# Attention in a hybrid block: later transposes, and operand splits spread over the query blocks

## The chip, the cores and the metric

The kernel runs on one core of a Trainium2 chip. The metric is the time of one execution in device microseconds (us). Three runs of the kernel before took 2177.57, 2182.42 and 2185.70 us; the median is 2182.42 us. A separate execution was profiled.

## The reference, cut to what matters

The block has a gated DeltaNet branch, an attention branch (MLA), a merge and a gated MLP. Only the attention's inner part bears on the change:

```python
# 8 heads, S = 1024 positions, keys of 128 + 64 channels, values of 128, f32
for s0 in range(0, S, 128):                      # 8 query blocks
    s1 = s0 + 128
    kb, vb = k[:, :s1], v[:, :s1]                # block-causal: keys up to s1
    sc = einsum('bqhd,bkhd->bhqk', q[:, s0:s1], kb) * scale
    sc = where(mask, sc, -inf)                   # mask by chunks of 64
    p = softmax(sc)
    outs.append(einsum('bhqk,bkhd->bqhd', p, vb))
```

## The kernel before, in words

All matrix products are done in a fast float32 form (fp32r) on operands that are split into a high and a low part. A product of two split operands takes three matmuls (high by high, high by low, low by high).

**The attention, in units.** A unit is one head and one query block of 128 rows. `units` lists, for each head, the blocks 6, 7, 0, 1, 4, 5, 2, 3 (`PAIRS`, L1200). For a unit with block i there are three jobs:

- `qk_ops` (L1212): scores, (i+1) x 128 columns wide, in PSUM banks of 512. Each bank takes five matmuls `s`: three over the 128 plain channels (`qnh`, `qnl`, `knh`, `knl`), two over the rotary channels (`qst` by `kst`, `qst` by `klo`). VectorE (DVE) takes the row maximum `nm` of each bank (L1233) and, with two banks, the smaller of the negated maxima (L1238). ScalarE (ACT) writes the exponentials into the SBUF tile `P` (L1240). DVE adds the row sums `sm` of two banks (L1242) and inverts them (L1243). GpSimd (POOL) multiplies `P` by the inverse (L136). There is one `P` tile for each of the eight blocks, and there are four score banks.
- `t_ops` (L1249): TensorE (PE) transposes `P` in chunks of up to four 128 x 128 tiles into a bank `pT` (L66). ACT copies the bank out as the high part `PTh` (L1263), DVE writes the low part `PTl` (L1264). There are two `pT` banks, so a chunk's transposes wait until the `PTl` of the chunk two before it is done.
- `pv_ops` (L1270): for a pair of blocks, the product with the values, matmuls `o`.

**Their order on PE** is written out by `attend`: step j issues the scores of unit j, the transposes of unit j - `LT`, and half of the value product of a pair whose last unit is `LT + LV` steps old. `LT` and `LV` are 4. A gate (`TD0`, `TD1`) keeps the transposes from being placed sooner than an assumed delay after their scores. `PEOrder` pins PE to that order. Each engine works through its own queue in order.

**The next head's operands.** While head h is under way, `attend` issues the loads for head h+1: `load_qk` for `kn`, `qn`, `kst`, `qst`, and `load_v`. `LJ` (L1177) says at which block of head h each of the four is issued; the entries are 0, 0, 0, 0, that is, all at the head's first step. Each load is a DMA on SP's queue into one of three raw buffers, and then a split: `knh`, `kst`, `qst` and `vh` are made by POOL (about 1 us each), `knl`, `qnl` and `vl` by POOL, `qnh` by ACT, and `klo` and the lower half of `qst` by DVE (L1192). The tiles of even heads have one buffer of each name, so `knh` of head 4 can be written only after head 2's last scores. For head 1 the entries are always 0, whatever `LJ` holds.

The order of the queues of DVE, ACT, POOL and SP is not the order of the program text: a scheduler places each instruction, and picks a raw buffer for each load, by its own estimates. It may place a split a whole head before the one that it is issued in.

Of the kernel before, what the change touches and what calls it, by code (L numbers as in the profile page):

```python
# [108 lines left out]
def build(tc, A, out):  # L109
    nc = tc.nc  # L110
    with ExitStack() as ctx:
        _body(tc, nc, ctx, A, out)


def _body(tc, nc, ctx, A, out):
# [1058 lines left out]
            nc.sync.dma_start(o(raw), src)  # L1174
        return raw

    LJ = (0, 0, 0, 0)  # L1177

    def load_qk(h, n):
        LOP = 3 if h != 1 else 0  # L1180
# [19 lines left out]
    PAIRS = (3, 0, 2, 1)  # L1200
    units = [(h, p, 2 * p + u) for h in range(NH) for p in PAIRS for u in range(2)]
    NU = len(units)
    LT = 4
    LV = 4
    TD0 = 3.5
    TD1 = 3e-3
# [3 lines left out]
    def qk_ops(j):  # L1210
        h, p, i = units[j]
        qc = slice(i * P, i * P + P)  # L1212
        W = (i + 1) * P
        nb = (W + 511) // 512
        d = hd[h]
        Pt = Pts[j] = pm.tile([P, W], F32, tag=f"P{i}", name=f"P{h}_{i}")
        nm = pm.tile([P, 2], F32, tag="nm", bufs=8, name=f"nm{h}_{i}")
        sm = pm.tile([P, 2], F32, tag="sm", bufs=8, name=f"sm{h}_{i}")
        ts = []

        def bank_op(b):
            w = min(512, W - b * 512)
            kc = slice(b * 512, b * 512 + w)
            t = bank("wk", f"s{h}_{i}_{b}")
            o = t[:, 0:w]
            pe.mm(o, d["qnh"][:, qc], d["knh"][:, kc], True, False)
            pe.mm(o, d["qnh"][:, qc], d["knl"][:, kc], False, False)
            pe.mm(o, d["qnl"][:, qc], d["knh"][:, kc], False, False)
            pe.mm(o, d["qst"][:, qc], d["kst"][:, kc], False, False)
            pe.mm(o, d["qst"][:, qc], d["klo"][:, kc], False, True)  # L1230
            if b == nb - 1:
                nc.vector.memset(t[0:64, w - 64:w], -1.0e30)
            nc.vector.tensor_reduce(nm[:, b:b + 1], o, axis=AX.X, op=ALU.max, negate=True)  # L1233
            ts.append((o, kc))
            if b < nb - 1:
                return
            if nb == 2:
                nc.vector.tensor_tensor(nm[:, 0:1], nm[:, 0:1], nm[:, 1:2], op=ALU.min)  # L1238
            for b, (o, kc) in enumerate(ts):
                nc.scalar.activation(Pt[:, kc], o, AF.Exp, bias=nm[:, 0:1], accum_out=sm[:, b:b + 1])  # L1240
            if nb == 2:
                nc.vector.tensor_tensor(sm[:, 0:1], sm[:, 0:1], sm[:, 1:2], op=ALU.add)  # L1242
            nc.vector.reciprocal(sm[:, 0:1], sm[:, 0:1])  # L1243
            gmul(Pt, Pt, sm[:, 0:1])
            pe.mark("QK", j)

        return [lambda b=b: bank_op(b) for b in range(nb)]

    def t_ops(j):  # L1249
        h, p, i = units[j]  # L1250
        n2 = j // 2
        u = i % 2
        if u == 0:
            PTs[n2] = [pm.tile([P, 2 * p + 2, 256], F32R, tag=f"PT{n}{p}", name=f"PT{n}{h}_{p}") for n in "hl"]
        PTh, PTl = PTs[n2]

        def chunk(k0):
            n = min(4, i + 1 - k0)
            t = bank("tp", f"pT{h}_{i}_{k0}")
            transposes(t, [Pts[j][:, (k0 + m) * P:(k0 + m + 1) * P] for m in range(n)])  # L1260
            tv = t[:, 0:n * P].rearrange("p (k c) -> p k c", c=P)
            dh = PTh[:, k0:k0 + n, u * P:(u + 1) * P]
            nc.scalar.copy(dh, tv)  # L1263
            nc.vector.tensor_tensor(PTl[:, k0:k0 + n, u * P:(u + 1) * P], tv, dh.bitcast(F32), op=ALU.subtract)  # L1264

        return [lambda k0=k0: chunk(k0) for k0 in range(0, i + 1, 4)]
# [36 lines left out]
    def attend():  # L1303
# [4 lines left out]
        pvq, nv = [], 1  # L1308
        for j in range(NU + LT + LV + 4):
            if j < NU:  # L1310
                h = units[j][0]
                if h == 1 and j % 8 == 0:
                    yield ((("ya",),), 0.0)
                for n, at in zip(("kn", "qn", "kst", "qst"), LJ if h else (0, 0, 0, 0)):
                    if h < NH - 1 and j % 8 == at:
# [3 lines left out]
            qs = qk_ops(j) if j < NU else []  # L1319
            ts = t_ops(j - LT) if 0 <= j - LT < NU else []  # L1320
            jv = j - LT - LV
            if 0 <= jv < NU and jv % 2 == 1:
# [5 lines left out]
            for r in range(n):  # L1328
# [6 lines left out]
                if r < len(ts):  # L1335
                    if r == 0:
                        yield ((("QK", j - LT),), TD0 + TD1 * (units[j - LT][2] + 1) * P)
                    ts[r]()
# [494 lines left out]
```

## Time and profile before

| | |
|---|---|
| median of three runs | 2182.42 us |
| the profiled execution | 2181.9 us |
| its span | 2180.2 us |
| PE busy in the span | 2085.7 us (96%) |
| DVE / ACT / POOL busy | 1334.7 / 903.8 / 735.2 us |
| attention: first scores of head 1 to last transposes after head 7's scores | 1128.26 to 1304.90 us |

The share of PE is an average over the whole block; the attention's stretch is read by itself in windows, one window to a head. A window starts with the head's first score matmul. A head's window also holds the previous head's transposes and value products, so that each whole head has the same work on PE.

### The profile page before, as it was taken

The page shows a single profiled execution, that of the slowest core. Times are in us where ns is not written, and L with a number is a line of the kernel's source. Part 1 is how long each engine was busy: PE and PEld are TensorE (multiplying, and loading weights), DVE is VectorE, ACT ScalarE, POOL GpSimd, SP SyncE. Part 2 cuts the span into 40 slices and gives each one's busy share as a digit, 9 for nine tenths or more (in the row PEclk, how much of TensorE's full clock was granted, in tenths as well). Part 3 has the DMA queues.
Part 4 walks back from the last instruction along what each step waited for, and adds up shares of the span by engine and source line. Part 5 has one row for each costly group of instructions (what it writes and reads, how often), then busy time and mean ns, then how long its engine had stood idle before and what let it go on. Part 6 is the DMA issues. An engine that isn't in the chain of part 4 may idle for free.

```text
span 2180.2 us, 30681 instructions
## 1 busy us (share of the span) xinstructions
PE 2085.7 (96%) x11526; PEld 1800.2 (83%) x11526; DVE 1334.7 (61%) x2214; ACT 903.8 (41%) x1822; POOL 735.2 (34%) x544
## 2 busy tenths in 40 slices
PE   6999999999999999889999999999999999999999
PEld 5878778888888899888778888898788888878887
DVE  7586798345565428677458885626665555564553
ACT  5666213443554423245136663246343433332222
POOL 1033320211101214447357760317544444442221
PEclk8999999999999999999999999999999999999999
DMA  9477523334333237687744427423322222344644
GB/s 272 124 196 197 147 88 131 90 90 125 107 117 93 82 111 240 201 299 243 237 146 130 126 69 256 131 88 97 111 93 78 87 87 87 95 143 145 222 146 148
DMA packets 277462, 309.31 MB, mean 142 GB/s; under 512 B 38896, under 2 KB 218429, under 8 KB 277057
## 3 DMA queue, kind: packets, MB, share of 16 engines
q1 hardware_dynamic: 277312, 307.35, 45.4%
q8 instruction: 91, 1.49, 0.3%
q14 instruction: 59, 0.48, 0.1%
HBM read 223.63 MB, written 83.66 MB: 141 GB/s over the span
## 4 chain that ended last, share of the span: by engine, by line
PE 70%; DVE 13%; DMA 8%; issue 3%; ACT 3%; POOL 3%; SPq 1%; ACTq 0%; DVEq 0%; POOLq 0%
PE d L63 11%; PE gt L63 5%; PE m L63 5%; PE my L63 5%; PE mx L63 5%; PE yb L63 4%; PE v L63 4%; PE wo L63 4%; PE qt L63 4%; PE q L63 3%; PE s L63 3%; PE mz L63 2%; PE ya L63 2%; DMA wada<-in_w_ada 2%; PE zt L63 2%
## 5 line engine op out<-in xcount | busy, mean ns | idle before, releaser
L63 PE MATMUL d<-wd,gh 128*128 128x512 f32 x704 | 217.5, 390 | 2.2 <-DVE wd L151 1.7
L63 PEld LDWEIGHTS d<-wd,gh 128*128 128x128 f32 x704 | 132.1, 188 | 30.7 <-DVE wd L151 2.5
L63 PE MATMUL d<-wd,gl 128*128 128x512 f32 x352 | 137.0, 389 | 0.0
L139 POOL TENSOR_TENSOR wdr<-wdr,gf 128x512 f32<-128x512 f32 x44 | 69.7, 1585 | 162.2 <-DMA wdr<-in_ffn_w_down 150.6
L151 DVE TENSOR_TENSOR gl<-gr,gh 128x1024 fp32r<-128x1024 f32 x44 | 56.3, 1281 | 109.7 <-ACT gh L143 107.6
L143 ACT CAST gh<-gr 128x1024 fp32r<-128x1024 f32 x44 | 46.3, 1054 | 153.4 <-PE d L63 152.9
L63 PEld LDWEIGHTS d<-wd,gl 128*128 128x128 f32 x352 | 66.1, 188 | 13.8
L1240 ACT ACTIVATE P<-s,nm 128x512 f32<-128x512 f32 (+2 forms) x96 | 55.3, 582 | 53.1 <-DVE nm L1238 44.4
L139 POOL TENSOR_TENSOR acc<-acc,vv 128x512 f32<-128x512 f32 x44 | 65.0, 1496 | 20.6 <-ACT acc L1768 20.6
L136 POOL TENSOR_SCALAR P<-P,sm 128x896 f32<-128x896 f32 (+4 forms) x64 | 49.7, 783 | 63.5 <-DVE nm L1238 16.7
L621 DVE TENSOR_TENSOR lt<-X 128x62 f32<-128x62 f32 (+30 forms) x62 | 61.6, 994 | 15.4 <-DMA X<-bd_d 13.3
L623 DVE TENSOR_TENSOR X<-X,lt 128x62 f32<-128x62 f32 (+30 forms) x62 | 61.8, 996 | 2.0
L1122 DVE SCALAR_TENSOR_TENSOR ada<-wada,sc,ada 128x1024 f32<-128x1024 f32 x28 | 42.5, 1518 | 32.7 <-DMA wada<-in_w_ada 32.6
L151 DVE TENSOR_TENSOR wd<-wdr,wd 128x512 fp32r<-128x512 f32 x44 | 61.2, 1392 | 1.8 <-ACT wd L143 1.8
L63 PE MATMUL mz<-T2h,wP 128*128 128x512 f32 x176 | 59.1, 397 | 3.1 <-ACT wP L143 2.1
L66 PE MATMUL pT<-ident,P 128*128 128x128 f32 x288 | 49.5, 282 | 12.7 <-DVE PTl L1264 9.6
L1263 ACT CAST PTh<-pT 128x512 fp32r<-128x512 f32 (+2 forms) x96 | 46.0, 484 | 37.6 <-PE pT L66 37.3
L63 PE MATMUL m<-B21h,wP 128*128 128x512 f32 x176 | 59.6, 400 | 0.0
L63 PE MATMUL mx<-B22h,wP 128*128 128x512 f32 x176 | 57.9, 390 | 0.0
L63 PE MATMUL my<-T4h,wP 128*128 128x512 f32 x176 | 57.8, 389 | 0.0
L63 PE MATMUL my<-T3h,wP 128*128 128x512 f32 x176 | 57.8, 389 | 0.0
L63 PE MATMUL m<-B11h,wP 128*128 128x512 f32 x176 | 57.5, 389 | 0.0
(1429 smaller groups left out, 7214.7 us busy)
## 6 DMA issues: line engine op xcount, KB each, us to landing
gr<-gg_d SPq DMA_DIRECT2D x44, 512.0 KB
wada<-in_w_ada SPq DMA_DIRECT2D x32, 512.0 KB
gg_d<-acc SPq DMA_DIRECT2D x22, 512.0 KB
wdr<-in_ffn_w_down SPq DMA_DIRECT2D x44, 256.0 KB
x<-in_x SPq DMA_DIRECT2D x16, 512.0 KB
ad<-in_w_ada SPq DMA_DIRECT2D x16, 512.0 KB
sg_d<-gst SPq DMA_DIRECT2D x32, 256.0 KB
q_d<-qst SPq DMA_DIRECT2D x48, 128.0 KB
```

What stands on the lines that cost most here:

```text
L63: self._pin(self.nc.tensor.matmul(out, lhsT, rhs, start=start, stop=stop, skip_group_check=more), cost)
L66: self._pin(self.nc.tensor.transpose(out=out, in_=in_, identity=ident), 0.107)
L136: return nc.gpsimd.tensor_scalar(o, i, by, 0.0, op0=ALU.mult, op1=ALU.add)
L139: nc.gpsimd.tensor_tensor(o, a, b, op=op)
L143: nc.scalar.copy(hi, src)
L151: return nc.vector.tensor_tensor(lo, src, hi.bitcast(F32), op=ALU.subtract)
L621: nc.vector.tensor_tensor(tv, X[:, 0:k, k:k + 1].broadcast_to([P, k, n]), X[:, k:k + 1, k + 1:64].broadcast_to([P, k, n]), op=ALU.mult)
L623: nc.vector.tensor_tensor(X[:, 0:k, k + 1:64], X[:, 0:k, k + 1:64], tv, op=ALU.add)
L1122: nc.vector.scalar_tensor_tensor(acc, raw, sc[:, k:k + 1], acc, op0=ALU.mult, op1=ALU.add)
L1240: nc.scalar.activation(Pt[:, kc], o, AF.Exp, bias=nm[:, 0:1], accum_out=sm[:, b:b + 1])
L1263: nc.scalar.copy(dh, tv)
```

## The change

`LJ` becomes 0, 1, 3, 5: of the next head's operands `kn` is issued at block position 0, `qn` at 1, `kst` at 3 and `qst` at 5. `LT` becomes 6: the transposes of a unit stand six steps behind its scores, and the value products, which hang on `LT + LV`, ten steps behind in place of eight.

```diff
-    LJ = (0, 0, 0, 0)
+    LJ = (0, 1, 3, 5)
@@
-    LT = 4
+    LT = 6
```

No instruction is added or removed on PE, DVE, ACT or POOL; all are the same in kind and number, and stand in another order.

On PE, from the opening of head 3 (`s3_6_0` is the first score bank of head 3, block 6; `pT2_4_0` the first chunk of head 2, block 4; the last matmul of each bank is shown). Before:

```order
L63 MATMUL s3_6_0_11079<-klo3_10729,qst3_10735 128x512
...
L66 MATMUL pT2_4_0_11089<-ident_73,P2_4_10902 128x128 x4
...
L63 MATMUL s3_7_0_11129<-klo3_10729,qst3_10735 128x512
...
L66 MATMUL pT2_5_0_11142<-ident_73,P2_5_10945 128x128 x4
...
L66 MATMUL pT2_2_0_11204<-ident_73,P2_2_10993 128x128 x3
```

Now:

```order
L63 MATMUL s3_6_0_11032<-klo3_10818,qst3_10909 128x512
...
L66 MATMUL pT2_0_0_11042<-ident_73,P2_0_10776 128x128
...
L63 MATMUL s3_7_0_11077<-klo3_10818,qst3_10909 128x512
...
L66 MATMUL pT2_1_0_11087<-ident_73,P2_1_10824 128x128 x2
...
L63 MATMUL s3_0_0_11114<-klo3_10818,qst3_10909 128x128
...
L66 MATMUL pT2_4_0_11128<-ident_73,P2_4_10863 128x128 x4
...
L66 MATMUL pT2_5_0_11178<-ident_73,P2_5_10915 128x128 x4
```

The wide score blocks 6 and 7 now stand beside the narrow transposes of blocks 0 and 1, and the wide transposes of 4 and 5 beside the narrow scores of 0 and 1.

On DVE in head 3, around the low half of head 4's `qst`. Before:

```order
L1264 TENSOR_TENSOR PTl2_2_11078<-pT2_5_0_11142,PTh2_2_11077 128x4x128
L1238 TENSOR_TENSOR nm3_7_11126<-nm3_7_11126 128x1
L1264 TENSOR_TENSOR PTl2_2_11078<-pT2_5_4_11169,PTh2_2_11077 128x2x128
L1232 MEMSET s3_0_0_11179 64x64
L1233 TENSOR_REDUCE nm3_0_11175<-s3_0_0_11179 128x1
L1192 TENSOR_TENSOR qst4_11068<-qstr4_11069,qst4_11068 64x1024
```

Now:

```order
L1238 TENSOR_TENSOR nm3_7_11074<-nm3_7_11074 128x1
L1192 TENSOR_TENSOR qst4_11242<-qstr4_11243,qst4_11242 64x1024
L1233 TENSOR_REDUCE nm3_0_11110<-s3_0_0_11114 128x1
L1232 MEMSET s3_1_0_11161 64x64
L1242 TENSOR_TENSOR sm3_7_11075<-sm3_7_11075 128x1
L1233 TENSOR_REDUCE nm3_1_11158<-s3_1_0_11161 128x1
L1243 RECIPROCAL sm3_7_11075<-sm3_7_11075 128x1
L1264 TENSOR_TENSOR PTl2_2_11113<-pT2_4_0_11128,PTh2_2_11112 128x4x128
```

`qst4` stood behind the copies of block 5's transposes; now the copies of blocks 4 and 5 stand behind it. Later in the same head DVE now also has head 5's `klo5` and `qst5`, the latter just ahead of the copies of blocks 6 and 7:

```order
L1233 TENSOR_REDUCE nm3_2_11284<-s3_2_0_11288 128x1
L1192 TENSOR_TENSOR qst5_11575<-qstr5_11576,qst5_11575 64x1024
L1264 TENSOR_TENSOR PTl3_3_11287<-pT3_6_0_11299,PTh3_3_11286 128x4x128
L1264 TENSOR_TENSOR PTl3_3_11287<-pT3_6_4_11310,PTh3_3_11286 128x3x128
```

In the kernel before they stand in head 4. On POOL, at the change from head 2 to head 3 (`P2_5` is the scaling of head 2, block 5). Before:

```order
L136 TENSOR_SCALAR knh4_11049<-knr4_11051 128x1024
L136 TENSOR_SCALAR kst4_11061<-kstr4_11063 128x1024
L136 TENSOR_SCALAR P2_2_10993<-P2_2_10993,sm2_2_10995 128x384
L139 TENSOR_TENSOR qnl4_11056<-qnr4_11057,qnh4_11055 128x1024
L139 TENSOR_TENSOR knl4_11050<-knr4_11051,knh4_11049 128x1024
L136 TENSOR_SCALAR P2_3_11023<-P2_3_11023,sm2_3_11025 128x512
L136 TENSOR_SCALAR qst4_11068<-qstr4_11069 128x1024
```

Now:

```order
L136 TENSOR_SCALAR knh4_11021<-knr4_11023 128x1024
L136 TENSOR_SCALAR P2_5_10915<-P2_5_10915,sm2_5_10917 128x768
L139 TENSOR_TENSOR knl4_11022<-knr4_11023,knh4_11021 128x1024
L136 TENSOR_SCALAR P2_2_10950<-P2_2_10950,sm2_2_10952 128x384
L136 TENSOR_SCALAR kst4_11150<-kstr4_11152 128x1024
L139 TENSOR_TENSOR qnl4_11068<-qnr4_11069,qnh4_11067 128x1024
L136 TENSOR_SCALAR P2_3_10983<-P2_3_10983,sm2_3_10985 128x512
L136 TENSOR_SCALAR qst4_11242<-qstr4_11243 128x1024
L136 TENSOR_SCALAR P3_6_11027<-P3_6_11027,sm3_6_11029 128x896
L136 TENSOR_SCALAR knh5_11354<-knr5_11356 128x1024
```

`kst4` moved behind `knl4`, and head 5's splits follow head 4's in the same head 3.

## Rows read from the trace of the kernel before

**Rows 1.** Heads 1 to 7, one window each: busy time of each engine, clock, DMA.
```profile
core 0: us, PE busy (x) PEld busy (x) DVE busy (x) ACT busy (x) POOL busy (x), PEclk, DMA share, GB/s
1128.26:1160.81 32.55, 25.46 (x151) 22.41 (x150) 27.15 (x51) 14.25 (x38) 26.34 (x20) 0.90 0.58 159
1160.81:1183.74 22.93, 22.16 (x160) 20.60 (x158) 18.99 (x51) 14.55 (x41) 12.61 (x12) 1.00 0.31 95
1183.74:1206.99 23.25, 22.13 (x160) 20.51 (x158) 20.38 (x46) 14.79 (x42) 22.89 (x17) 1.00 0.54 152
1206.99:1231.98 24.99, 22.44 (x160) 20.57 (x158) 21.29 (x56) 14.46 (x41) 14.01 (x15) 1.00 0.42 113
1231.98:1255.16 23.18, 22.06 (x159) 20.46 (x158) 20.31 (x46) 14.81 (x42) 22.60 (x17) 1.00 0.52 153
1255.16:1282.95 27.79, 24.07 (x159) 21.95 (x158) 24.42 (x53) 15.54 (x40) 23.14 (x18) 0.94 0.41 120
1282.95:1304.90 21.95, 21.95 (x160) 20.49 (x158) 17.04 (x59) 14.42 (x44) 7.21 (x10) 1.00 0.01 2
```

**Rows 2.** Waits of PE's matmuls, 1132 to 1310 us: total, times, longest.
```profile
PE pT L66 <- DVE PTl L1264: 9.6, 8, 1.8
PE s L63 <- DVE qst L1192: 3.3, 1, 3.3
PE pT L66 <- DVE sm L1243: 2.3, 1, 2.3
```

**Rows 3.** PE in order of time: transposes that started late, in brackets the wait.
```profile
1143.65 0.52 PE L66 MATMUL pT<-ident,P 128*128 128x128 f32 x3 [0.82 <-DVE PTl L1264]
1148.97 0.63 PE L66 MATMUL pT<-ident,P 128*128 128x128 f32 x4 [2.25 <-DVE sm L1243]
...
1218.84 0.52 PE L66 MATMUL pT<-ident,P 128*128 128x128 f32 x3 [1.84 <-DVE PTl L1264]
...
1267.08 0.52 PE L66 MATMUL pT<-ident,P 128*128 128x128 f32 x3 [1.83 <-DVE PTl L1264]
...
1271.97 0.63 PE L66 MATMUL pT<-ident,P 128*128 128x128 f32 x4 [1.82 <-DVE PTl L1264]
```

**Rows 4.** PE in order of time in head 3, without waits: the spacing of matmuls.
```profile
1199.70 0.39 PE L63 MATMUL s<-knh,qnl 128*128 128x512 f32 x1
1199.93 0.40 PE L63 MATMUL s<-kst,qst 128*128 128x512 f32 x1
...
1202.39 0.28 PE L63 MATMUL o<-PTh,vl 128*128 128x256 f32 x1
1202.51 0.60 PE L66 MATMUL pT<-ident,P 128*128 128x128 f32 x4
1202.86 0.42 PE L63 MATMUL s<-knh,qnh 128*128 128x384 f32 x1
```

**Rows 5.** DVE in order of time, heads 1, 3 and 4.
```profile
1146.64 1.72 DVE L1192 TENSOR_TENSOR klo<-kstr,kst 128x1024 fp32r<-128x1024 f32 x1
...
1150.12 3.37 DVE L1192 TENSOR_TENSOR qst<-qstr,qst 64x1024 fp32r<-64x1024 f32 x1
...
1194.15 1.25 DVE L1192 TENSOR_TENSOR qst<-qstr,qst 64x1024 fp32r<-64x1024 f32 x1
...
1213.69 3.43 DVE L1192 TENSOR_TENSOR qst<-qstr,qst 64x1024 fp32r<-64x1024 f32 x1
...
1218.02 0.67 DVE L1264 TENSOR_TENSOR PTl<-pT,PTh 128x512 fp32r<-128x512 f32 x1
```

**Rows 6.** POOL in order of time, heads 1, 3 and 4.
```profile
1150.04 2.37 POOL L139 TENSOR_TENSOR knl<-knr,knh 128x1024 fp32r<-128x1024 f32 x1
...
1200.29 1.04 POOL L136 TENSOR_SCALAR knh<-knr 128x1024 fp32r<-128x1024 f32 x1
...
1213.64 2.39 POOL L139 TENSOR_TENSOR vl<-vr,vh 128x1024 fp32r<-128x1024 f32 x1
1218.28 1.02 POOL L136 TENSOR_SCALAR P<-P,sm 128x896 f32<-128x896 f32 x1 [2.24 <-DVE sm L1243]
```

**Rows 7.** DVE and POOL by line and shape, 1128 to 1317 us: busy, mean ns.
```profile
L1192 DVE TENSOR_TENSOR qst<-qstr,qst 64x1024 fp32r<-64x1024 f32 x7 | 16.4, 2344 | 0.2
...
L1192 DVE TENSOR_TENSOR klo<-kstr,kst 128x1024 fp32r<-128x1024 f32 x7 | 10.5, 1505 | 0.9 <-POOL kst L136 0.9
...
L136 POOL TENSOR_SCALAR P<-P,sm 128x768 f32<-128x768 f32 x7 | 6.4, 917 | 8.9 <-PE s L63 4.6 <-DVE PTl L1264 2.3 <-ACT P L1240 1.9
...
L136 POOL TENSOR_SCALAR P<-P,sm 128x512 f32<-128x512 f32 x7 | 4.9, 694 | 2.4 <-DVE sm L1243 1.5 <-PE s L63 0.8
...
L136 POOL TENSOR_SCALAR P<-P,sm 128x384 f32<-128x384 f32 x7 | 4.2, 598 | 0.0
```

## The prediction

> **What bounds the kernel now.** The table of busy times comes first: PE is busy for 2085.7 us of a span of 2180.2 us. So PE bounds the block, and what can be won in the attention is PE's idle time or a lower granted clock there, nothing else, since the change adds and removes no matmul. The second view is the windows, one to a head [rows 1]. Head 7, which has no loads for a next head beside it, takes 21.95 us with PE busy for all of 21.95 us: that is the work of one head on PE at clock 1.00. The other heads stand above it by 10.60, 0.98, 1.30, 3.04, 1.23 and 5.84 us (heads 1 to 6), 22.99 us in all. Heads 1 and 6, the two dear ones, also show a clock of 0.90 and 0.94, and PE "busy" longer for the same matmuls.
>
> The third view is the waits of PE [rows 2]. Almost all stand at the transposes `pT`, and the engine waited for is DVE: 9.6 us in 8 waits for `PTl` (a bank of `pT` not yet free) and 2.3 us for a row sum. One wait of another kind, 3.3 us at score matmuls `s` for the low half of `qst`, is head 1's opening: head 1's own operands are not ready when its scores begin. The list in order of time places the others: two in head 1 (0.82 and 2.25 us), one in head 4 (1.84), two in head 6 (1.83 and 1.82) [rows 3]. DVE's list says what DVE did meanwhile [rows 5]: `klo` (1.72 us) or the low half of `qst`, which takes 1.25 us in head 3 and 3.37 and 3.43 us in heads 1 and 4. POOL's list has the difference [rows 6]: in the two long cases POOL began a split of two operands (`knl` 2.37 us, `vl` 2.39 us) within 0.1 us of it. So the bound in this stretch is the order of DVE's queue: a long split stands ahead of a short `PTl` for which PE waits.
>
> **The change part by part.** Both edits only reorder. The splits are the same seven `klo` and seven `qst` (means 1505 and 2344 ns [rows 7]), and PE has the same 21.95 us of work to a head.
>
> *Head 1 as a receiver.* Its own loads are issued as before, so its opening wait of 3.32 us stays. Of the 22.99 us, 22.99 - 3.32 = 19.67 us can be reached at most.
>
> *Transposes two blocks later.* A bank of scores has about two units more until its `P` is wanted. That speaks for the loss of waits for a row sum (2.25 us in head 1), since `sm` then has two units more to be late in. It does not help a wait for `PTl`, because that is a matter of two transposes that share a bank, and the distance between those is set by what PE does between them. PE's order now puts the wide transposes of blocks 4 and 5 beside the narrow scores of blocks 0 and 1, where little PE work stands between; the narrow transposes, which need little of DVE, stand beside the wide scores. Evacuation is spread more evenly, slack is not.
>
> *Operands spread over blocks 0, 1, 3 and 5.* By the new order of DVE, head 1 has `klo2` and `qst2`, head 2 `klo3` and `qst3`, head 3 two of each (for heads 4 and 5), head 4 only `klo6` at its end, head 5 `qst6` and `klo7`, head 6 `qst7`. So head 3 gets more than it had, head 4 and head 6 less.
>
> *Head 3 worked out.* POOL's new row from head 2's last scores to the high half of `qst4` is `knh` 1.04, `P` of 768 columns 0.92, `knl` 2.37, `P` of 384 0.60, `kst` (taken like `knh`) 1.04, `qnl` (taken like `knl`) 2.37, `P` of 512 0.69, `qst` (like `knh`) 1.04: together 10.07 us [rows 6, 7]. The first of them waits for head 2's last scores, since head 4 uses head 2's buffer. Between those scores and head 3's first, PE has nine `o` at 0.12 and two chunks of transposes at 0.35, 1.78 us [rows 4]. `qst4`'s high half is therefore there 10.07 - 1.78 = 8.29 us into head 3. DVE then adds its low half: 1.25 us alone [rows 5], or, if it must sit out the scaling of `P` by 1.02 us that follows on POOL [rows 6], 2.27 us. Then, behind it, the short reductions and the `PTl` of block 4; in head 4 of before, 0.90 us lie between the end of `qst` (1213.69 + 3.43) and the start of `PTl`, which takes 0.67 us [rows 5]. The bank comes free at 8.29 + 1.25 + 0.90 + 0.67 = 11.1 us at the least, 12.1 us at the most. PE wants it for block 5's transposes after 15 score matmuls of 512 columns at 0.23, five of 384 at an estimated 0.18 (by width), ten narrow ones at an estimated 0.12 (no less than an `o`), 27 `o` at 0.12 and eight transposes at 0.35/4: 3.45 + 0.90 + 1.20 + 3.24 + 0.70 = 9.5 us into the head [rows 4]. The wait is 1.6 to 2.6 us; I take 2.0, which also lies by the 1.83 and 1.84 us of [rows 3]. `qst5`, later in the same head, stands directly ahead of the `PTl` of blocks 6 and 7, and I give it the same 2.0. Head 3: 4.0 us above 21.95, where it was 1.30.
>
> On the two ends of that wait the rows show 1.25 us alone and 3.43 us beside `vl` of 2.39 us [rows 5, 6]. The Trainium skill, "SBUF — State Buffer", section "Who interferes with whom", says that an exclusive lock on a port pair shared by DVE and GpSimd is the only such contention: whichever holds it keeps the other out. With 1.25 + 2.39 = 3.64 us the trace roughly agrees, and by the rule the dearer end, 2.6 us, would hold, so head 3 would stand at 5.2 and the sum would be 1.2 us less favourable.
>
> *The other heads.* Head 1: 10.60 - 3.32 = 7.28; the waits of 0.82 and 2.25 us lie at transposes that now stand elsewhere, and I let both go: 4.2. I let the rest stay, since `qst2` on POOL is still followed by `knh3` and the 2.37 us of `knl3`, so that DVE's half of it stays long. Head 2 keeps one `klo` and one `qst`: 1.0. Head 4 loses its loads but for `klo6`, so it becomes like head 2: 1.0 in place of 3.04. Head 5 has `qst6` and `klo7` in an order that I cannot place against the waits; between its 1.23 and head 3's 4.0 I take the middle, 2.6. Head 6 loses `klo7` and with it one of its two waits, 5.84 - 1.83 = 4.0. Head 7: 0. Each of these lies between 0 (head 7) and 5.84 us (head 6), the nearest rows for a head with little and with much to wait for, and I keep these as its bounds.
>
> The sum is 4.2 + 1.0 + 4.0 + 1.0 + 2.6 + 4.0 + 0 = 16.8 us against 19.67, so -2.9 us. The tail behind head 7 has two more units of transposes and value products in it, but these were PE work inside the heads before; I set it at nothing, and if PE waited there once like in [rows 3] it would be +1.8. The profiled execution took 2181.9 us; with -2.9 it would be 2179.0. The median of the runs is 2182.42, 0.5 us above it, and on that scale the forecast is 2179.5 us.
>
> **The rivals.**
>
> *The splits disappear behind PE (big gain).* If later transposes leave DVE enough room everywhere, heads 1 to 6 fall to head 2's 0.98: 6 x 0.98 = 5.9 us, a gain of 19.67 - 5.9 = 13.8 us, 2182.4 - 13.8 = 2168.6 us; at the very best 2162.7. For it: head 2, with one `klo` and one `qst`, shows that a head can carry its loads at nearly no price [rows 1], and so does head 3 of before with its `qst` of 1.25 us. Against it: head 3 now has two loads, and wide transposes with little PE work between them.
>
> *The operands come late (slower).* The new order puts `klo` and `qst` early in DVE's queue and their POOL halves late in POOL's. DVE works in order; if it comes to `qst` before POOL has made the high half, everything behind it stands, the `nm` without which the exponentials cannot start as well as the `PTl` for which PE waits. In head 3 POOL's half is there at 8.3 us by the working above, and a raw buffer that comes free late, or a DMA that lands late, would push that out. It decides once `qst` is more than some 4 us later than worked out (a wait of 2.0 + 4 is head 6's excess of 5.84). If then each of heads 1 to 6 costs what head 6 does now, they cost 35.0 us, +15.4 against 19.67: 2197.8 us. For it: both stalls that come in a row in head 6 drop the clock to 0.94 [rows 1]. Against it: before, waits of `klo` for POOL's half come to 0.9 us in all [rows 7], so POOL has been ahead.
>
> *The change does nothing here.* The waits only change places and their sum stays: 2182.4 us. For it: no split is taken away or shortened, and the list of them in DVE is as long as before.
>
> **How the numbers follow.** The forecast of 2179.5 has 0.58; its own range is 2172 to 2188, from the bounds of heads 3, 5 and 6 (about 7 us down, 8 up). The big gain has 0.16, the late operands 0.16, no effect 0.10. A measurement can tell some 0.5% from no change, 10.9 us here. The big gain lies beyond that, and so do the late operands; the other two are within: 0.16 faster, 0.68 the same, 0.16 slower. The range leaves out a tenth on each side: 2168 to 2191 us.
>
> **What would show it.** In windows by head: head 3 grows from 23.25 to about 26, head 4 falls to about 23, head 6 to about 26, head 2 and head 7 stay, head 1 falls to about 29.5 and still has 3.3 us of waiting for `qst` at its opening. In PE's waits: `pT` on `PTl` remains the largest, now at block 5's first chunk and at blocks 6 or 7 in head 3; `pT` on `sm` is gone. Heads 3 and 5 without such a wait would be the big gain. A wait of DVE for POOL's `kst` or `qst` of more than 1 us, or a score matmul that waits for `klo` or `qst` in a head past the first, would be the late operands. The mean of `qst` on DVE (2344 ns) should change little. I am wrong if the sum over the heads falls by over 10.9 us or rises at all by more than one wait of [rows 3].

## The result: slower by 0.8%

The changed kernel took 2201.39 us (median of 4 runs, 2198.08 to 2206.43), beside 2184.06 us for the kernel before (4 runs, 2177.57 to 2186.39). The ratio is 1.0076, 95% interval 1.0054 to 1.0099: 17 us slower, where 2.9 us of gain were forecast. The profiled execution has a span of 2196.3 us against 2180.2.

### The profile after

The attention holds the loss. From head 1's first scores to the start of the next stage (`yb`) it took 1315.30 - 1128.26 = 187.04 us before and 1332.60 - 1131.69 = 200.91 us now, 13.9 us more. What lies ahead of it takes 3.4 us more, all of it before head 0's first scores, and what lies behind it 1.2 us less; PE's order is unchanged in both, and the runs of the kernel before alone differ by 8.8 us. Windows of the changed kernel, heads 1 to 6 and then head 7 up to `yb` (columns as in [rows 1]):

```profile
core 0: us, PE busy (x) PEld busy (x) DVE busy (x) ACT busy (x) POOL busy (x), PEclk, DMA share, GB/s
1131.69:1162.39 30.70, 23.61 (x136) 20.81 (x135) 25.93 (x51) 14.10 (x38) 23.10 (x17) 0.89 0.59 161
1162.39:1186.67 24.28, 22.57 (x159) 20.59 (x158) 20.13 (x50) 14.07 (x42) 18.00 (x17) 1.00 0.42 121
1186.67:1215.25 28.58, 24.28 (x160) 22.03 (x158) 22.57 (x53) 14.71 (x43) 21.01 (x18) 0.94 0.54 159
1215.25:1240.83 25.58, 22.61 (x160) 20.64 (x158) 17.19 (x48) 14.55 (x42) 14.10 (x14) 1.00 0.23 70
1240.83:1267.91 27.08, 23.89 (x160) 21.90 (x158) 20.98 (x51) 14.32 (x41) 20.45 (x17) 0.94 0.56 156
1267.91:1295.98 28.07, 22.79 (x159) 20.71 (x158) 21.56 (x49) 16.55 (x44) 20.75 (x16) 1.00 0.25 76
1295.98:1332.60 36.62, 34.52 (x262) 32.47 (x260) 24.03 (x71) 20.59 (x58) 8.13 (x11) 1.00 0.08 27
```

The same stretch of head 7 before:

```profile
1282.95:1315.30 32.35, 31.88 (x244) 30.24 (x242) 22.72 (x71) 19.61 (x58) 8.11 (x11) 1.00 0.09 28
```

Against [rows 1], head 2 grew by 1.35 us, head 3 by 5.33, head 4 by 0.59, head 5 by 3.90, head 6 by 0.28. Heads 1 and 7 belong together (their windows exchange PE work, since the backlog is two units longer): 30.70 + 36.62 against 32.55 + 32.35, 2.42 more. Of the 13.9 us, 9.8 are idle time of PE (26.65 against 16.84), 4.1 are longer busy time. The waits of PE in the attention of the changed kernel (total, times, longest):

```profile
PE pT L66 <- DVE PTl L1264: 19.7, 14, 2.9
PE pT L66 <- DVE s L1232: 2.9, 3, 1.3
PE s L63 <- DVE qst L1192: 2.9, 1, 2.9
```

Waits of `pT` for `PTl` doubled from 9.6 us in 8 to 19.7 in 14 [rows 2]; the opening of head 1 is nearly what it was. In PE's order of time, eight of the transposes that started late (the wait in brackets), in this order block 5 of head 2, blocks 7 and 5 of head 3, blocks 7 and 5 of head 4, block 5 of head 5, blocks 7 and 5 of head 6, each the first chunk of its block:

```profile
1199.58 0.63 PE L66 MATMUL pT<-ident,P 128*128 128x128 f32 x4 [2.42 <-DVE PTl L1264]
...
1213.71 0.63 PE L66 MATMUL pT<-ident,P 128*128 128x128 f32 x4 [1.49 <-DVE PTl L1264]
...
1225.90 0.63 PE L66 MATMUL pT<-ident,P 128*128 128x128 f32 x4 [0.93 <-DVE PTl L1264]
...
1239.14 0.63 PE L66 MATMUL pT<-ident,P 128*128 128x128 f32 x4 [1.26 <-DVE s L1232]
...
1253.97 0.63 PE L66 MATMUL pT<-ident,P 128*128 128x128 f32 x4 [2.93 <-DVE PTl L1264]
...
1279.96 0.63 PE L66 MATMUL pT<-ident,P 128*128 128x128 f32 x4 [2.10 <-DVE PTl L1264]
...
1294.40 0.63 PE L66 MATMUL pT<-ident,P 128*128 128x128 f32 x4 [2.62 <-DVE PTl L1264]
...
1306.65 0.63 PE L66 MATMUL pT<-ident,P 128*128 128x128 f32 x4 [0.93 <-DVE PTl L1264]
```

In the fourth the profile names a memset that stands directly behind the `PTl` in DVE's queue. The last lies inside head 7's window, where no split of a next head is under way. So what is late there is not a split. The chain of that last wait, in the changed kernel, first PE:

```profile
1303.40 0.60 PE L66 MATMUL pT<-ident,P 128*128 128x128 f32 x4
```

then ACT:

```profile
1303.51 0.69 ACT L1240 ACTIVATE P<-s,nm 128x512 f32<-128x512 f32 x1 [1.95 <-DVE nm L1238]
...
1304.18 0.68 ACT L1240 ACTIVATE P<-s,nm 128x512 f32<-128x512 f32 x1
...
1304.85 0.37 ACT L1240 ACTIVATE P<-s,nm 128x128 f32<-128x128 f32 x1
...
1305.19 0.59 ACT L1263 CAST PTh<-pT 128x512 fp32r<-128x512 f32 x1
```

then DVE:

```profile
1305.82 0.69 DVE L1264 TENSOR_TENSOR PTl<-pT,PTh 128x512 fp32r<-128x512 f32 x1
```

The first chunk of block 4's transposes was done at 1304.00, but ACT first wrote the exponentials of block 7 and block 0, whose scores PE had just made, and came to `PTh` at 1305.19. `PTl` ended at 1306.51, 3.1 us after the start of block 4's transposes. PE wanted the bank again for block 5 at 1306.65 - 0.93 = 1305.72, only 2.3 us after that start: beside these transposes stand only narrow scores and `o`. The same two blocks before, PE in head 7:

```profile
1284.53 0.60 PE L66 MATMUL pT<-ident,P 128*128 128x128 f32 x4
...
1288.16 0.60 PE L66 MATMUL pT<-ident,P 128*128 128x128 f32 x4
```

There 3.63 us lie between the two starts, most of them matmuls of wide scores, and a delay of 3.1 us would be hidden.

### The profile page after: what moved, and what is told of

The parts are those of the page before. It is cut to its first block, busy times and chain, and to the rows that moved or that the text cites. A ratio compares the mean times of both kernels' runs of the same rounds, so it can differ in the third digit from the quotient of the medians.

```text
span 2196.3 us, 30702 instructions
## 1 busy us (share of the span) xinstructions
PE 2085.3 (95%) x11526; PEld 1797.6 (82%) x11526; DVE 1337.7 (61%) x2214; ACT 902.9 (41%) x1822; POOL 728.6 (33%) x544
## 3 DMA queue, kind: packets, MB, share of 16 engines
q8 instruction: 91, 1.49, 0.3%
## 4 chain that ended last, share of the span: by engine, by line
PE 67%; DVE 11%; DMA 7%; POOL 3%; issue 2%; ACT 2%; SPq 1%; POOLq 0%; ACTq 0%; DVEq 0%
PE d L63 11%; PE gt L63 6%; PE mx L63 5%; PE my L63 5%; PE m L63 4%; PE qt L63 4%; PE yb L63 4%; PE v L63 4%; PE wo L63 4%; PE q L63 3%; PE s L63 3%; PE mz L63 2%; PE o L63 2%; PE zt L63 2%; DVE X L623 2%
## 5 line engine op out<-in xcount | busy, mean ns | idle before, releaser
L66 PE MATMUL pT<-ident,P 128*128 128x128 f32 x288 | 49.1, 281 | 23.1 <-DVE PTl L1264 19.7
L621 DVE TENSOR_TENSOR lt<-X 128x62 f32<-128x62 f32 (+30 forms) x62 | 59.5, 960 | 15.3 <-DMA X<-bd_d 13.3
L1233 DVE TENSOR_REDUCE nm<-s 128x1 f32<-128x512 f32 (+2 forms) x96 | 52.7, 551 | 11.9 <-PE s L63 11.0
L1264 DVE TENSOR_TENSOR PTl<-pT,PTh 128x512 fp32r<-128x512 f32 (+2 forms) x96 | 51.6, 548 | 12.9 <-ACT PTh L1263 12.3
```

The source lines that it names most:

```text
L66: self._pin(self.nc.tensor.transpose(out=out, in_=in_, identity=ident), 0.107)
L621: nc.vector.tensor_tensor(tv, X[:, 0:k, k:k + 1].broadcast_to([P, k, n]), X[:, k:k + 1, k + 1:64].broadcast_to([P, k, n]), op=ALU.mult)
```

## The experiments

Each kernel was timed beside runs of the kernel before on the same chip; medians of that are 2183.1, 2182.9, 2183.4, 2182.6 and 2183.7 us in the five sets. "Heads 2 to 6" is the sum of their five windows in the kernel's own profile: 122.2 us before, 133.6 in the changed kernel. One execution of each was profiled, and it can lie off the median (`lt8`: 2181.4 us, `after_nosplit`: 2201.6); the time ahead of head 0's first scores, whose matmuls no edit touches, runs from 1101.1 to 1112.3 us in these profiles. So profiles are compared by the attention alone. A name with `_nosplit` has DVE's `klo` and `qst` work of heads 2 to 7 left out.

| kernel | us | ratio to before, 95% | heads 2 to 6 |
|---|---|---|---|
| lt6_only | 2208.8 | 1.0115, 1.0099 to 1.0131 | 142.8 |
| lj_only | 2193.7 | 1.0041, 1.0025 to 1.0056 | 129.3 |
| before_nosplit | 2173.7 | 0.9953, 0.9936 to 0.9969 | 116.0 |
| after_nosplit | 2197.8 | 1.0065, 1.0047 to 1.0084 | 131.4 |
| lj_nosplit | 2174.9 | 0.9962, 0.9950 to 0.9974 | 117.0 |
| wide4_nosplit | 2190.5 | 1.0032, 1.0014 to 1.0051 | 124.1 |
| lt6_pairs_nosplit | 2181.1 | 0.9995, 0.9983 to 1.0007 | 119.2 |
| lt8_nosplit | 2172.3 | 0.9952, 0.9933 to 0.9971 | 114.5 |
| pth_dve_nosplit | 2187.0 | 1.0022, 1.0007 to 1.0036 | 125.4 |
| low_on_pool | 2186.6 | 1.0020, 1.0008 to 1.0032 | 125.9 |
| after_bank3 | 2193.9 | 1.0044, 1.0026 to 1.0062 | 135.8 |
| before_bank3 | 2191.4 | 1.0040, 1.0025 to 1.0055 | 129.7 |
| quarters_pinned | 2205.6 | 1.0103, 1.0083 to 1.0123 | 138.4 |
| after_pairs | 2197.7 | 1.0064, 1.0040 to 1.0088 | 138.7 |
| locks_apart | 2180.7 | 0.9992, 0.9978 to 1.0007 | 120.8 |
| after_locks | 2194.0 | 1.0044, 1.0031 to 1.0058 | 131.9 |
| lt8 | 2189.5 | 1.0027, 1.0012 to 1.0041 | 125.4 |
| lt8_locks | 2189.7 | 1.0025, 1.0012 to 1.0038 | 129.1 |

### Which half of the change

`lt6_only` is the kernel before with

```diff
-    LT = 4
+    LT = 6
```

> Transposes six steps behind, operands issued at block 0 as in the kernel before. Theory A (the new pairing of transposes with scores leaves too little matmul time beside the transposes of blocks 5 and 7, in every head): nearly all of the loss is here, 2184 + 13 to 17 = 2197 to 2201 us, PE waits for PTl about 20 us in the attention, at blocks 5 and 7 in heads 2 to 7, also in head 7 which has no loads. Theory B (the loads spread over the blocks put klo and qst at bad places of DVE's queue): this alone does no harm, 2180 to 2186 us.

`lj_only`:

```diff
-    LJ = (0, 0, 0, 0)
+    LJ = (0, 1, 3, 5)
```

> Operands issued at blocks 0, 1, 3, 5, transposes four steps behind as in the kernel before. Theory A: within 4 us of before, 2180 to 2188 us. Theory B: the loss is here, 2197 to 2201 us, with stalls of heads 3 and 5 as in the changed kernel.

Measured: +25.7 and +10.5 us over the 2183.1 of that set, where both together cost 17.3. The later transposes are the larger part, as theory A has it, but 2208.8 lies above its 2197 to 2201, the spread alone is not free (A expected within 4 us), and together they cost 19 us less than the sum. In `lj_only` DVE comes to a `qst` before POOL has made its high half, and a transpose waits behind it:

```profile
1256.63 2.03 DVE L1192 TENSOR_TENSOR qst<-qstr,qst 64x1024 fp32r<-64x1024 f32 x1 [2.33 <-POOL qst L136]
```

```profile
1260.83 0.63 PE L66 MATMUL pT<-ident,P 128*128 128x128 f32 x4 [3.81 <-DVE PTl L1264]
```

That is the forecast's rival of late operands, in a kernel other than the one it was made for. In `lt6_only` the same place in head 3 as in the changed kernel costs PE twice as much; DVE, POOL and PE there:

```profile
1198.42 3.16 DVE L1192 TENSOR_TENSOR qst<-qstr,qst 64x1024 fp32r<-64x1024 f32 x1
```

```profile
1198.15 2.35 POOL L139 TENSOR_TENSOR vl<-vr,vh 128x1024 fp32r<-128x1024 f32 x1
```

```profile
1203.70 0.66 PE L66 MATMUL pT<-ident,P 128*128 128x128 f32 x2 [4.91 <-DVE PTl L1264]
```

In the changed kernel `qst` at this place takes 1.22 us, since the spread moved POOL's row and no `vl` is under way beside it, and the wait is 2.42 us. By the profiles, that is where the two halves make up for each other: heads 3, 5 and 6 take 94.9 us in `lt6_only` and 28.58 + 27.08 + 28.07 = 83.7 in the changed kernel, 11.2 us apart; over the whole attention, from head 0's first scores to `yb`, the two are 9.9 us apart (235.3 and 225.4).

### With and without DVE's splits

```diff
+        if h >= 2:
+            return                  # DVE's low part is not made
...
+        if n == "kst" and h >= 2:
+            d["klo"] = hd[0]["klo"]
```

> The changed kernel without DVE's low parts of the next heads' operands: for heads 2 to 7 klo is not made (head 0's stands in) and qst keeps its high part in both halves; 12 DVE instructions of 1.25 to 3.4 us are gone, the rest is unchanged. Theory A: each of heads 2 to 7 still loses what head 7 loses more in the changed kernel, 2.3 us, so this stands 14 to 16 us above the kernel before without the same instructions. Theory B: 0 to 3 us above it. Theory C (the pairing narrows the slack, and a split in DVE's queue uses it up; each alone costs little): 2 to 6 us above it.

> The kernel before with the same 12 DVE instructions left out (klo and the low half of qst for heads 2 to 7). All theories: heads 2 to 7 come near head 7's 21.95 us, so the heads' excess of about 23 us falls to some 10 (head 1's opening and what is left there), 2168 to 2175 us. It is the base for the run before this one.

Measured: 2197.8 against 2173.7, 24 us apart; more than A's 14 to 16, and far from B and C. Of the changed kernel's 2201.4 the splits are 3.6 us. The loss is not the place of DVE's splits.

POOL's `knl`, `qnl` and `vl` are still made in these two kernels, and DVE's small instructions still meet them. In head 6 of `after_nosplit`, DVE and then POOL:

```profile
1291.78 2.29 DVE L1242 TENSOR_TENSOR nm<-nm 128x1 f32<-128x1 f32 x1
```

```profile
1291.67 2.38 POOL L139 TENSOR_TENSOR vl<-vr,vh 128x1024 fp32r<-128x1024 f32 x1
```

The exponentials, `PTh` and `PTl` come late behind this `nm`, and block 7's transposes wait 3.17 us. More such meetings are not the difference: the `nm` and `sm` of this one-column kind together take 28.0 us of DVE in `after_nosplit` and 31.5 in `before_nosplit`. But where they fall beside narrow matmuls they may lengthen a wait; no run leaves POOL's splits out, so their part in the 24 us stays open.

`lj_nosplit` is the kernel before without splits, with `LJ = (0, 1, 3, 5)`.

> The operands spread over blocks 0, 1, 3, 5 with transposes four behind, and the 12 DVE splits left out. If the 10.5 us that the spread alone cost come from the place of klo and qst in DVE's queue: as the kernel before without them, 2172 to 2177 us. If they come from the place of POOL's splits and of the DMAs: 2181 to 2186 us.

2174.9 us beside 2173.7: at four steps, nearly all of the spread's own cost goes through `klo` and `qst`.

### Pairing or distance

```diff
-    PAIRS = (3, 0, 2, 1)
+    PAIRS = (3, 2, 1, 0)            # wide4_nosplit, LT = 4
...
+    PAIRS = (3, 2, 0, 1)            # lt6_pairs_nosplit, after_pairs, LT = 6
...
+    LT = 8                          # lt8_nosplit, lt8, old PAIRS
```

> Like the kernel before without the 12 DVE splits (2173.7 us), transposes four steps behind as there, but the pairs of blocks in the order 6,7,4,5,2,3,0,1. That puts scores 0,1 beside transposes 4,5 and scores 2,3 beside transposes 6,7, as in the changed kernel. Theory A (the pairing costs): the stalls at blocks 5 and 7 appear in every head at a distance of four, 2186 to 2196 us. Theory D (the distance of six costs, since a block's P has one buffer and only two steps are left until it is written again): no change, 2172 to 2176 us.

> Like the changed kernel without the 12 DVE splits (2197.8 us), transposes six behind, but the pairs in the order 6,7,4,5,0,1,2,3: scores 6,7 now stand beside transposes 4,5 and scores 0,1 beside 2,3, as in the kernel before; scores 2,3 still stand beside transposes 6,7. Theory A: the stalls at block 5, 10.9 us over the heads, go, those at block 7 stay, 2184 to 2190 us. Theory D: no change, 2195 to 2200 us.

> Like the kernel before without the 12 DVE splits (2173.7 us), but transposes eight steps behind: scores 6,7 stand beside transposes 6,7 of the head before, 0,1 beside 0,1, 4,5 beside 4,5. Theory A (the pairing alone): wide beside wide again, 2172 to 2180 us in spite of the greater distance. Theory D (the distance, through the single buffer of each block's P, which is now written and transposed in one step): above the 2197.8 us of six steps, 2198 to 2215 us. In between would give both a part.

At six steps the other order of pairs gave back 16.7 us (2197.8 to 2181.1), somewhat more than forecast; in the profiles the attention, from head 0 on, is shorter by as much (224.1 to 207.4), and no wait at block 5 is left in heads 1 to 6. At four steps the bad pairing cost 16.8 us (2173.7 to 2190.5), a number as theory A has it, but not by the stalls that it named: in the profile the attention carries only 9.2 of it (201.9 to 211.1), waits for `PTl` come to 1.3 us, and PE waits most for row sums:

```profile
PE pT L66 <- DVE sm L1247: 7.7, 11, 2.9
```

So the sign of that run speaks for the order of the pairs; that it acts through the banks is not shown at four steps. Eight steps, where each block's transposes stand beside the same block's scores, cost nothing: 2172.3 us, with an attention of 202.3 against 201.9. PE's largest wait there:

```profile
PE pT L66 <- DVE PTl L1268: 5.5, 8, 1.1
```

against this in `after_nosplit`:

```profile
PE pT L66 <- DVE PTl L1268: 14.2, 11, 2.9
```

A distance of 4, 6 and 8 gives 2173.7, 2197.8 and 2172.3 us (the second with the spread, which at four steps costs nothing without splits). Distance as such, theory D, is out.

With the splits in place:

> The kernel before with transposes eight steps behind in place of four, nothing left out. By the pairing alone (the same blocks of two heads side by side): as good as four, 2178 to 2184 us. If the place of DVE's splits in the new order falls badly, as with the other order of pairs at six: 2188 to 2198 us.

> The changed kernel, nothing left out, with the pairs in the order 6,7,4,5,0,1,2,3, so that scores 6,7 stand beside transposes 4,5. Theory A: as without the splits, where the same edit gave 16.7 us back: 2201.4 - 16.7 = 2184.7, 2181 to 2189 us. If DVE's splits fall as badly there as with the old pairs: 2190 to 2200 us.

2189.5 at eight steps, against 2208.8 at six and 2183.7 at four: the same sequence, but eight now costs 5.8 us. `after_pairs` gave back only 3.7 us of 2201.4, and in its profile the attention is not shorter (227.7 against 225.4). Its waits moved to the scores:

```profile
PE s L63 <- ACT P L1240: 17.6, 11, 5.1
```

The longest of them, in head 3, followed back: PE had no bank for scores until ACT had read one, ACT waited for a maximum `nm`, and on DVE that `nm` stood behind `qst` and then beside POOL's `knl`. PE, ACT, DVE and POOL:

```profile
1202.55 0.80 PE L63 MATMUL s<-knh,qnh 128*128 128x512 f32 x1 [5.15 <-ACT P L1240]
```

```profile
1201.72 0.69 ACT L1240 ACTIVATE P<-s,nm 128x512 f32<-128x512 f32 x1 [1.68 <-DVE nm L1238]
```

```profile
1197.67 1.74 DVE L1192 TENSOR_TENSOR qst<-qstr,qst 64x1024 fp32r<-64x1024 f32 x1
...
1199.76 1.87 DVE L1238 TENSOR_TENSOR nm<-nm 128x1 f32<-128x1 f32 x1
```

```profile
1198.42 3.19 POOL L139 TENSOR_TENSOR knl<-knr,knh 128x1024 fp32r<-128x1024 f32 x1
```

Theory A's size was wrong here: with the splits in place the good pairing alone does not bring the time back, and in this head they fall badly in its order.

### ACT's queue, and the banks

```diff
-            nc.scalar.copy(dh, tv)
+            if (i, k0) in ((4, 0), (6, 0)):
+                nc.vector.tensor_copy(dh, tv)
+            else:
+                nc.scalar.copy(dh, tv)
```

> The changed kernel without the 12 DVE splits (2197.8 us), and the high copies PTh of the first chunks of blocks 4 and 6 made by DVE in place of ACT. Theory A' (those copies are late because they stand in ACT's queue behind the exponentials of scores that PE has only just made): the stalls of 1.1 us and more at blocks 5 and 7 fall, 2184 to 2192 us. Rival (there is too little matmul time beside them, whichever engine copies): 2195 to 2201 us.

2187.0, 10.8 us less than `after_nosplit`, though DVE got 16 copies more. Waits for `PTl` fell from 14.2 to 8.9 us. In head 3, block 5 starts without a wait, where `after_nosplit` waited 0.92 us (in other heads block 5 still waits up to 1.9 us); DVE and then PE of this run:

```profile
1215.56 0.69 DVE L1268 CAST PTh<-pT 128x512 fp32r<-128x512 f32 x1 [0.36 <-PE pT L66]
1216.29 0.69 DVE L1271 TENSOR_TENSOR PTl<-pT,PTh 128x512 fp32r<-128x512 f32 x1
```

```profile
1217.13 0.63 PE L66 MATMUL pT<-ident,P 128*128 128x128 f32 x4
```

So ACT's order makes a good part of the lateness (A'), 10.8 of the 24 us; 13.3 us above `before_nosplit` are left that this run does not place.

```diff
-            t = bank("tp", f"pT{h}_{i}_{k0}")
+            t = bank("wk" if (i, k0) in ((7, 0), (1, 0), (5, 0), (3, 0)) else "tp", f"pT{h}_{i}_{k0}")
```

> The changed kernel with a third bank for the transposes: the first chunks of blocks 7, 1, 5 and 3 take a bank of the scores' ring of four. Theory A (a chunk waits for the bank of the chunk two before it, whose copies are late): the stalls at blocks 5 and 7 go, 2184 to 2192 us. Rival: the scores wait for their lent bank in turn and the loss only moves, 2198 us or more.

> The same third bank in the kernel before. Theory A: waits of a transpose for PTl there come to 9.6 us, some of them at block 2 and 6, which keep their two banks; 2178 to 2184 us. If the scores' ring is what suffers: 2186 to 2195 us.

The changed kernel gained 7.5 us, between the two forecasts; the kernel before lost 8.0, as forecast if the scores' ring suffers. In the former the waits at the transposes fell to a few us, and the scores took over:

```profile
PE s L63 <- ACT P L1240: 10.6, 5, 3.2
```

The two banks are where the delay is felt; a third, lent from the scores, gives back less than half of the 17 us, and new waits for score banks stand in its place.

### What the splits themselves are worth

`low_on_pool` makes `klo` and the low half of `qst` of heads 2 to 7 on POOL:

```diff
-        LOP = 3 if h != 1 else 0
+        LOP = 15 if h > 1 else 3 if h == 0 else 0
```

> The kernel before with klo and the low half of qst of heads 2 to 7 made by POOL in place of DVE. If DVE's queue is what PE waits for and POOL has room (it is busy 7 to 26 us of a head's 22 to 33): up to the 9.4 us that leaving them out gave, 2174 to 2180 us. If POOL's added 2.4 us instructions keep DVE's small reductions waiting: 2184 to 2200 us.

`quarters_pinned` issues them in quarters:

```diff
+        for c in range(0, S, 256 if h >= 2 else S):
...
+            if j % 8 in (3, 4, 5, 6):
+                for low in lows[:2]:
+                    follow(low(), lastl[0], True)
+                del lows[:2]
```

> The kernel before with each klo and each low half of qst of heads 2 to 7 cut into four DVE instructions of 256 columns, two pinned behind the last PTl of each of the steps 3 to 6 of a head. If the length of a split in DVE's queue is what PE waits for: a good part of the 9.4 us that leaving the splits out gave, 2174 to 2180 us. If the place matters more than the length, or POOL's halves come too late for these places: 2183 us or more.

2186.6 and 2205.6: neither gives the 9.4 us that leaving them out gave. Why `low_on_pool` stays above the kernel before was not followed. The quarters came too late; score matmuls waited for `qst` at the opening of heads 2, 4, 6 and 7 too, not of head 1 alone (3.3 of this row, as before):

```profile
PE s L63 <- DVE qst L1194: 12.6, 5, 4.0
```

`locks_apart` and `after_locks` let POOL's `knl`, `qnl` and `vl` wait for `qst` (`lt8_locks` has the same at eight steps):

```diff
+    def apart(h):
+        return (lambda ins: follow(ins, lowq[h])) if h in lowq and h >= 2 else nc.gpsimd
...
-            split(d[n + "h"], d[n + "l"], raw, heng, nc.gpsimd if LOP & (1 if n == "kn" else 2) else None)
+            split(d[n + "h"], d[n + "l"], raw, heng, apart(h - 1) if LOP & (1 if n == "kn" else 2) else None)
...
-        split(d["vh"], d["vl"], raw, nc.gpsimd, nc.gpsimd)
+        split(d["vh"], d["vl"], raw, nc.gpsimd, apart(max(lowq)))
```

> The kernel before with one more wait: from head 2 on, POOL's two-operand splits knl, qnl of a later head and vl wait until DVE has made the low half of the qst before them, so that the two do not meet. If the meeting (3.4 us in place of 1.25) is what the split costs: the mean of qst falls from 2344 towards 1300 ns and heads 4 and 6 lose less, 2176 to 2181 us. If POOL's chain becomes late by it, or the small reductions of DVE are hit in its place: 2183 us or more.

> The same wait in the changed kernel. Its splits cost only some 3.6 us there (2201.4 against 2197.8 without them), so 2197 to 2202 us; below 2195 us would mean that the meetings, not the pairing, make the loss; above 2204 us that POOL is late by the wait.

> The same, with POOL's knl, qnl and vl waiting for the low half of qst as in locks_apart. If a long split in DVE's queue is still what is waited for at eight steps: 1 to 6 us under the run before this one, 2174 to 2182 us. If not: equal to it within 2 us.

In the kernel before the mean of `qst` fell to 1288 ns, and the time did not move beyond the noise (2180.7, inside the first range forecast, but the interval holds 1). Head 6 lost less than before (25.97 against 27.79 us), head 4 did not (25.00 against 24.99). Head 4 shows why; DVE of `locks_apart`, then POOL:

```profile
1215.51 1.22 DVE L1197 TENSOR_TENSOR qst<-qstr,qst 64x1024 fp32r<-64x1024 f32 x1
...
1216.95 2.36 DVE L1251 TENSOR_TENSOR sm<-sm 128x1 f32<-128x1 f32 x1
```

```profile
1216.91 2.38 POOL L149 TENSOR_TENSOR vl<-vr,vh 128x1024 fp32r<-128x1024 f32 x1 [1.47 <-PE pT L66]
```

`qst` is short, and a `TENSOR_TENSOR` on a single column, which takes 0.14 us in head 7, sits out `vl` in its place. The transpose behind it waits 1.88 us, where it waited 1.84 [rows 3]. At eight steps the same wait gave nothing (2189.7). After the change it gave 7.4 us: 2194.0 lies under the 2195 that was to speak for the meetings as the cause. The profile does not bear that out. From head 1 to `yb` it is 5.8 us shorter, and 4.0 of these are head 1 (26.71 against 30.70 us, with a clock of 1.00 in place of 0.89); heads 2 to 6 gained 1.7, and block 5's transposes in head 3 wait longer than the 2.42 us of the changed kernel:

```profile
1194.53 0.80 PE L66 MATMUL pT<-ident,P 128*128 128x128 f32 x4 [4.84 <-DVE PTl L1273]
```

No version tried with the whole computation is faster than the kernel before beyond the noise.

## Why the prediction was wrong

**What bounds.** Right: PE's idle time at `pT`, released by DVE, was and is the largest part of the attention's loss.

**Head 3 worked out.** The two waits came near, 2.42 and 1.49 us where 1.6 to 2.6 and 2.0 were forecast, but the first in part by luck, since its chain was another. POOL's high half of `qst4` was there at 1194.30, 7.6 us into the head (head 3 began at 1186.67), earlier than the 8.29 forecast. POOL, then DVE, then ACT:

```profile
1193.25 1.05 POOL L136 TENSOR_SCALAR qst<-qstr 128x1024 fp32r<-128x1024 f32 x1
```

```profile
1196.31 1.22 DVE L1192 TENSOR_TENSOR qst<-qstr,qst 64x1024 fp32r<-64x1024 f32 x1
...
1198.77 0.86 DVE L1264 TENSOR_TENSOR PTl<-pT,PTh 128x512 fp32r<-128x512 f32 x2
```

```profile
1197.71 0.58 ACT L1263 CAST PTh<-pT 128x512 fp32r<-128x512 f32 x1
```

DVE came to it only at 1196.31, after `nm`, and block 4's `PTh` ended on ACT at 1198.29, after `qst` was done. So `PTl` began 12.1 us into the head, where the sum gives 10.4 to 11.5, and PE wanted the bank at 1199.58 - 2.42 = 1197.16, 10.5 us in, where the sum gives 9.5: both ends were late, and the difference stayed. The head as a whole stands 6.6 us above 21.95, not 4.0. Its waits come to 4.3 (0.39 for a score bank among them), and 2.3 are longer busy time of PE, for which the sum has no term. Most of that is the clock: in windows of 1 us it is 0.70, 0.50, 0.50 and 0.59 from 1200 to 1204, some 1.7 us of work at full clock lost.

**The step that failed** is "Transposes two blocks later", with its consequence "Head 7: 0" and "Head 4: 1.0". I saw that the transposes of 4 and 5 now have little PE work between them and gave that a price only where a split stood in DVE's queue. The delay that the runs show needs no such split: `PTh` waits in ACT's queue behind the exponentials of scores just made, and PE is back at the bank before `PTl` is done. It costs 0.93 us at block 5 in the windows of heads 4 and 7, with no split on DVE near, and with DVE's splits of heads 2 to 7 left out the changed kernel still stood 24 us above the kernel before. In head 4, set at 1.0 above 21.95, waits alone come to 2.98 us. The kernel before had a sign of it: two waits of 1.12 us, in heads 3 and 5, that are not in the list of [rows 3]. At the one in head 3, PE and then ACT:

```profile
1197.58 0.63 PE L66 MATMUL pT<-ident,P 128*128 128x128 f32 x4 [1.12 <-DVE PTl L1264]
```

```profile
1195.37 1.00 ACT L1263 CAST PTh<-pT 128x384 fp32r<-128x384 f32 x2
```

Block 2's transposes were done at 1193.92; ACT wrote three exponentials and a copy of `o` first, and came to this `PTh` at 1195.37.

**Head by head** the miss is 1.3 us in head 2, 2.6, 2.6, 2.5 and 2.1 in heads 3 to 6, and 5.5 in heads 1 and 7 together, 16.7 of the 13.9 + 2.9 = 16.8 us. That it is so even is chance: in head 4 it is mostly waits, in heads 3 and 5 mostly longer busy time (2.3 and 1.9 us) at a clock of 0.94. The range has a slip of its own: with 0 and 5.84 as bounds of heads 3, 5 and 6 it would reach 10.6 us down and 6.9 up, not 7 and 8; the result lies outside both.

**A wait for `sm` goes.** Right: the 2.3 us of [rows 2] have no row after.

**The mean of `qst` changes little.** Wrong: 2344 ns before [rows 7], 1744 after, while the time rose. On the rule that was weighed in head 3's sum: the Trainium skill, "SBUF — State Buffer", section "Who interferes with whom", has DVE and GpSimd exclude each other on a shared port pair. The rows of `locks_apart` agree for the meeting (2.36 beside 2.38 us). In head 3 the dearer end did not hold: `qst` began 0.08 us before POOL's `knh` and took 1.22 us, and `knh` took 2.05 in place of 1.04 [rows 6]. What the forecast lacked is that parting two of them can let a third meet.

**The rival of late operands** named 2197.8 us, but by another mechanism. DVE waits for POOL's halves by 0.6 us in all in the changed kernel, no score matmul past head 1's opening waits for `qst`, and heads 3 to 5 cost far from the same. It is seen in `lj_only` and, at the scores, in `quarters_pinned`.

**Still open:** whether some order of the splits brings six steps with the good pairing down to the kernel before (`after_pairs` has the only one tried); what POOL's splits add to the waits without DVE's; and how the 16.8 us of `wide4_nosplit` divide, of which its attention shows 9.2.

## What to carry to other kernels

When software pipelining is deepened by k steps, what changes is not only the distance but which work stands beside which: put the wide evacuations beside the wide matmuls, and check the distance against the period of the work (here the wide pairs stand four steps apart, so 4 and 8 match and 6 does not). That held without DVE's splits of the next heads; with them eight steps still cost 5.8 us. Price a new order first on the part of the kernel that has nothing else under way, here head 7, by following each bank through every engine that copies it, ACT's queue included. A wait that is measured at one instruction is not won by shortening that instruction, if the next in the queue meets the same obstacle, as in head 4 of `locks_apart`.

## What was not expected of the hardware

A DVE `TENSOR_TENSOR` on one column took 2.36 us beside a POOL subtraction of 2.38 us, 1.87 beside one of 3.19, and 0.14 us in head 7 with none beside it: in these rows the size of an instruction did not protect it. After PE's waits of 2.42 us in head 3 and 2.93 in head 5 of the changed kernel, windows of 1 us show the granted clock at 0.50, the lower level of 1.2 GHz, and at 1.00 again within some 5 us of the wait's end. Heads 2 and 4, whose waits stay under 1.4 us, show 1.00 throughout; but so does head 6, with waits of 2.10 and 2.62 us, so the length of a wait alone does not tell.
